# Two low-rank inputs transposed later in the projection phase, and modulation weights fetched one chunk earlier

## The chip, the core and the metric

The kernel runs on one core of one Trainium2 chip. The metric is device microseconds from start to end of one execution. The core has five instruction queues that run side by side, each strictly in its own order: PE (TensorE, matrix products and transposes), DVE (VectorE), ACT (ScalarE), POOL (GpSimd) and SP (SyncE, which here only issues transfers). They wait for one another through semaphores.

## What is computed

Two layers of a transformer over 512 latent tokens and 256 context tokens (768 rows, six tiles of 128) with 1024 features. The part that matters here is the input projection of a layer and what is made of its columns:

```
h  = modulate(rms_norm(x, g_norm_attn[l]), sh1, sc1)
lat = prep_stream(h @ w_in[l], rope_mla, rope_hd, *group_params)
# in prep_stream:
q_lat, kv_lat, k_pe, sq, sk, sv, dq, dk, dv, ga, gb, gc = split_columns(proj)
mq = (rms_norm(q_lat, g_q_lora) @ w_uq)
kv = (rms_norm(kv_lat, g_kv_lora) @ w_ukv)
sq = rms_norm(sq, g_swa_q); sk = rms_norm(sk, g_swa_k)      # then rope
dq = rms_norm(dq, g_diff_q); dk = rms_norm(dk, g_diff_k)    # then rope
```

After it come attention in three branches, a gated merge and an MLP. In the second (last) layer only the 512 latent rows are queries, so four tiles, not six, are made of each query group. The modulation vectors are `silu(c) @ w_mod + b_mod`.

## The kernel before

All products are kept at float32 accuracy by splitting each factor in a high and a low part and adding three products, so each (tile, 128-row slice of the weights) costs three matrix instructions. `piece` fetches weights into a staging tile `wr` (two buffers, on SP), ACT writes the high part `wh` (L197) and POOL the low part `wl` (L201). `bproj` (L473) runs the three products (L483, L484, L485) into an accumulator `pb`; ACT copies each finished tile out.

Each layer's phase 1 first computes the narrow columns, among them `rkv` (kv_lat) and `rq` (q_lat). Then `lora(rkv)` and `lora(rq)` are written in the code, ahead of all further chunks: ACT squares the rows (L464), DVE sums them (L465), forms the inverse root in some ten small dependent instructions (L445 to L456), scales the rows (L470); PE transposes the tiles into `pt` (L612; six to each 128 columns in the first layer for `rkv`, twelve for `rq`; six and eight in the second layer); ACT and DVE split the result into `lh` and `ll` (L615, L616). `kvT` and `qT`, these results, are what the low-rank products of `ukv` and `uq` read.

After that a string (L762) gives the order of the chunks, one letter each:

- a, c, g, i, m, n are `qk_chunk`: 256 columns of the big projection, 24 matrix instructions to a tile (144 for six tiles, 96 for four), then on DVE a sum of squares, the rotation with POOL's help (L505 to L512), the inverse root and the scaling, then a store to memory.
- e, k are `dvc`, the same size with no work after it. b, h, f, l are `ukv`: 3 instructions to a tile, 18 in all, reading `kvT`. d, j are `uq`: 6 instructions of 384 columns to a tile, reading `qT`.
- P starts the next phase (attention), whose first transposes `tp` read tiles `ld` that were stored and fetched back (`km`, `qm`).

In the first layer `mod_units(2)` runs after every letter: it fetches two weight tiles `wm` (SP, L308) and at once multiplies them (`pm`, L268) into a shared accumulator; every second call ends a group, which ACT copies (`me`), PE transposes (L276) and DVE adds up (L316).

The order on each engine is not the order of the code. A scheduler sets it ahead of time, from priorities that follow the order of the code and from tile dependencies; the code's order decides which instruction comes first where several are ready in its model, and in which order accumulator buffers are handed out. Accumulators `pb` alternate between two tags of two buffers each; `pt` and `pm` share a tag of two buffers. On the chip each engine then follows its fixed order: a waiting instruction holds up all behind it.

Of the kernel before, what the change touches and what calls it, by code (L numbers as in the profile page):

```python
# [14 lines left out]
F32 = mybir.dt.float32  # L15
# [30 lines left out]
P_GA, P_GM, P_BM, P_GQ, P_GKV, P_GS = 0, 8, 16, 64, 66, 67  # L46
# [90 lines left out]
class Build:  # L137
# [161 lines left out]
    def mod_units(self, n):  # L299

        nc = self.nc
        for _ in range(n):
            if self.mu == 24:
                return
            u, i = self.mu // 4, self.mu % 4
            self.mu += 1
            w = self.ph.tile([128, 1024], F32, tag="wm", bufs=self.NM, name=self.nm("wm"))
            nc.sync.dma_start(w, self.ins["wm1"][u, i])  # L308
            if i == 0:
                self.mps = self.psS("pm")  # L310
            self.mod_pe(w, (2 * i, 2 * i + 1), self.mps)
            if i == 3:
                v = self.mod_out(self.mps, self.mps[:, 512:640])
                o = (2, 4, 3)[u // 2] * 8 + u % 2 * 4
                for s in range(2):
                    nc.vector.scalar_tensor_tensor(out=self.mod[0][s][:, o:o + 4], in0=v[:, :, s], scalar=0.5,  # L316
                                                   in1=self.vp[0][:, P_BM + o:P_BM + o + 4], op0=ALU.mult, op1=ALU.add)
# [197 lines left out]
    def phase1(self, l, h, nq, pre):  # L515
# [102 lines left out]
                res.append((hi, lo))  # L618
            return res

        kvT = lora(rkv, 1, 6, P_GKV)

        ss = self.sumsq(rsk, 12, 64)
        self.rope_pairs(rsk, 1, 6, tabs["sk"], gains["sk"])
# [42 lines left out]
                nc.sync.dma_start(d, raw[:, a * nt * 128:(a + 1) * nt * 128])  # L667
                sc.setdefault(key, []).append(d)

        qT = lora(rq, 2, nq, P_GQ)  # L670

        kw = []

# [85 lines left out]
                 h=lambda: ukv(1), i=lambda: qk_chunk(2, qt, "sq", "qs"), j=lambda: uq(1), k=lambda: dvc(8),  # L759
                 l=lambda: ukv(3), m=lambda: qk_chunk(3, qt, "dq", "qd"), n=lambda: qk_chunk(4, qt, "dq", "qd"))  # L760

        for f in ("mcafldebghijnPk", "abcdjehmflgnikP")[l]:  # L762
            if f == "P":
                self.early = True
                for _ in job[0]():
                    pass
                self.early = False
                continue
            F[f]()
            if l == 0:  # L770
                self.mod_units(2)
# [591 lines left out]
    def build(self):  # L1363
        tc, nc, ins = self.tc, self.nc, self.ins
        import contextlib
        with contextlib.ExitStack() as es:
            self.kp = es.enter_context(tc.tile_pool(name="kp", bufs=1))
            self.sp = es.enter_context(tc.tile_pool(name="sp", bufs=1))
            self.pp = es.enter_context(tc.tile_pool(name="pp", bufs=1, space=bass.MemoryType.PSUM))
            self.dr = es.enter_context(tc.tile_pool(name="dr", bufs=1, space=bass.MemoryType.DRAM))  # L1370
            self.NS, self.WR, self.WH = 25, 2, 4
            kp = self.kp
            self.kc = kp.tile([128, NK], F32, name="kc")
            self.ident = self.kc[:, K_ID:K_ID + 128]
            self.vp, self.vb, self.mod, self.modr, self.lam, self.gsub, self.sink = [], [], [], [], [], [], []
            for l in range(DEPTH):
                self.vp.append(kp.tile([128, NP_], F32, name=f"vp{l}"))
                self.mod.append([kp.tile([128, 48], F32, name=f"mod{l}{s}") for s in range(2)])
                self.modr.append([kp.tile([128, 48], F32, name=f"modr{l}{s}") for s in range(2)])

            nc.scalar.preload_act_table_set("exp_and_others")

            cp, ct = self.tiny("cp", 64)[:, 0:16], self.tiny("cq", 64)[:, 0:16]
            nc.sync.dma_start(cp, ins["cp"])
            nc.scalar.activation(out=ct, in_=cp, func=AF.Tanh, scale=0.5)
            sl = self.sl = kp.tile([128, KT, 32], F32, name="sl")
            nc.vector.memset(sl, 0.0)
            nc.vector.scalar_tensor_tensor(out=sl[:, :, 0:2], in0=ct.rearrange("p (k s) -> p k s", s=2), scalar=1.0,
                                           in1=cp.rearrange("p (k s) -> p k s", s=2), op0=ALU.add, op1=ALU.mult)
            nc.sync.dma_start(self.kc[:, 0:K_COS], ins["kc"][:, 0:K_COS])  # L1390
            self.identr = kp.tile([128, 128], F32R, name="identr")
            nc.scalar.activation(out=self.identr, in_=self.ident, func=AF.Copy)
            nc.sync.dma_start(self.vp[0], ins["vp"][0])
            x = []
            for k in range(KT):
                t = self.S("x")
                nc.sync.dma_start(t, ins["xT"][k])
                x.append(t)
            xd = [ins["xT"][k] for k in range(KT)]
            with self.phase("p0", NPB=3):  # L1400
                h = self.norm_tiles()
                qps = self.first_norm(x, h)
            nc.sync.dma_start(self.kc[:, K_COS:NK], ins["kc"][:, K_COS:NK])
            nc.sync.dma_start(self.vp[1], ins["vp"][1])
            for l in range(DEPTH):
                nq = 6 if l < DEPTH - 1 else 4
                n = nq * 128
                with self.phase("p1", ND=5, NPB=3, NM=2):
                    self.layer_consts(l)
                    if l == 0:  # L1410
                        self.mu = 0
                    sc, job, st = self.phase1(l, h, nq, qps if l == 0 else pre)
                m = [None] * 8
                with self.phase("p2", ND=4, NPB=4, NL=3, NR=6, NG=3):
                    ys, gates = self.phase2(l, h, sc, nq, job, st)
                    yh = self.y_split(ys, 0, n)
                    yh = self.merge(l, 0, ys, yh, gates, m, nq, self.psd)
                with self.phase("p3", NR=16, NPB=2, NL=2, NG=4, NM=1):
                    yh = self.merge(l, 1, ys, yh, gates, m, nq, self.psx)
                    mh = self.merge(l, 2, ys, yh, gates, m, nq, self.psx)  # L1420
                    if l == 0:
                        self.silu = []
                        for s in range(2):
                            cb, t = (self.tiny(q, 64)[:, 0:8] for q in ("cb", "ct"))
                            nc.sync.dma_start(cb, ins["cc"][s].rearrange("(p q) -> p q", q=8))
                            nc.scalar.activation(out=t, in_=cb, func=AF.Tanh, scale=0.5)
                            nc.vector.scalar_tensor_tensor(out=t, in0=t, scalar=1.0, in1=cb, op0=ALU.add, op1=ALU.mult)
                            d = self.dr.tile([1024], F32, name=f"silu{s}")
                            nc.sync.dma_start(d.rearrange("(p q) -> p q", q=8), t)
                            self.silu.append(d)  # L1430
                    x = []
                    for k in range(KT):
                        t = self.S("x")
                        nc.sync.dma_start(t[:, :n], xd[k][:, :n])
                        x.append(t)
                    h2 = self.norm_tiles()
                    pre = self.out_proj(l, mh, x, nq, lambda acc, c: self.norm(l, 1, x, acc, h2, c, l == 0 and c.start >= LAT))
                with self.phase("p4", NR=16, NPB=3, NM=2):
                    if l == 0:
                        self.mod_start([(0, 5, (0, 1)), (1, 1, (0, 1)), (1, 0, (0, 1))]  # L1440
                                       + [(1, kd, (0,)) for kd in (2, 4, 3, 5)])
                        acc = self.S("acc1")
                        hn = self.norm_tiles()
                        xd = [self.dr.tile([128, 512], F32, name=self.nm("xd")) for _ in range(KT)]

                        def fin(j, c):
                            sq = self.ph.tile([128, 1024], F32, tag="wm", bufs=self.NM, name=self.nm("sq"))
                            self.add_square(acc, x[j], j, c, sq, nc.vector if j > 5 else nc.gpsimd)
                            if c.stop == LAT:
                                nc.sync.dma_start(xd[j], x[j][:, 0:LAT])  # L1450

                        def done(c):
                            self.norm(1, 0, x, acc, hn, c)
                    else:
                        def fin(j, c):
                            nc.sync.dma_start(self.out[j][:, c], x[j][:, c])

                        def done(c):
                            pass
                    pre = self.mlp(l, h2, x, nq, pre, fin, done)  # L1460
                    if l == 0:
                        h = hn
# [69 lines left out]
```

## Time and profile before

| | |
|---|---|
| median of three runs | 2515.46 us (2514.19 to 2516.1) |
| profiled execution | 2519.05 us, span of its instructions 2517.3 us |
| PE busy | 2425.4 us, 96% of the span |
| DVE, ACT, POOL busy | 60%, 43%, 44% |
| mean granted TensorE clock | 0.992 |
| phase 1, first layer | about 60 to 300 us |
| phase 1, second layer | about 1497 to 1700 us |

Times in the trace are counted from the span's first instruction. "Idle before" in brackets is how long the engine had stood still when that instruction began, and after the arrow what it waited for. Windows give each engine's busy time in a stretch and the granted clock as a share of full speed (1.00 is 2.4 GHz).

### The profile page before, as it was taken

The page shows a single profiled execution, that of the slowest core. Times are in us where ns is not written, and L with a number is a line of the kernel's source. Part 1 is how long each engine was busy: PE and PEld are TensorE (multiplying, and loading weights), DVE is VectorE, ACT ScalarE, POOL GpSimd, SP SyncE. Part 2 cuts the span into 40 slices and gives each one's busy share as a digit, 9 for nine tenths or more (in the row PEclk, how much of TensorE's full clock was granted, in tenths as well). Part 3 has the DMA queues.
Part 4 walks back from the last instruction along what each step waited for, and adds up shares of the span by engine and source line. Part 5 has one row for each costly group of instructions (what it writes and reads, how often), then busy time and mean ns, then how long its engine had stood idle before and what let it go on. Part 6 is the DMA issues. An engine that isn't in the chain of part 4 may idle for free. (4 is left out here: it accounts for less than half of the span.)

```text
span 2517.3 us, 40953 instructions
## 1 busy us (share of the span) xinstructions
PE 2425.4 (96%) x15466; PEld 2132.4 (85%) x15466; DVE 1498.0 (60%) x3081; ACT 1078.8 (43%) x2105; POOL 1102.9 (44%) x1423
## 2 busy tenths in 40 slices
PE   7999999999999999899999989999999999999999
PEld 6899888888888888788888889988888778888888
DVE  5547677778883468872222266777788874522222
ACT  4344466667662233222222234446677643422221
POOL 3534321221116438664444464562222247556654
PEclk9999999999999999999999999999999999999999
DMA  7265422222336315671111122542323354222222
GB/s 277 97 209 209 140 96 92 82 79 96 103 131 213 126 66 176 212 250 68 59 68 61 66 84 90 193 145 90 115 79 111 118 170 161 84 100 93 93 100 84
DMA packets 133190, 307.45 MB, mean 122 GB/s; under 512 B 43264, under 2 KB 49536, under 8 KB 132608
## 3 DMA queue, kind: packets, MB, share of 16 engines
q1 hardware_dynamic: 122624, 281.23, 32.9%
q10 hardware_dynamic: 10368, 23.60, 2.4%
q8 instruction: 122, 2.00, 0.3%
q14 instruction: 76, 0.62, 0.1%
HBM read 252.08 MB, written 52.70 MB: 121 GB/s over the span
## 5 line engine op out<-in xcount | busy, mean ns | idle before, releaser
L201 POOL TENSOR_TENSOR wl<-wr,wh 128x256 fp32r<-128x256 f32 x1060 | 847.2, 828 | 1014.5 <-ACT wh L197 959.4
L197 ACT ACTIVATE wh<-wr 128x1024 fp32r<-128x1024 f32 (+2 forms) x266 | 279.9, 1052 | 629.6 <-PE mo L221 310.0
L220 PE MATMUL mo<-uh,wh 128*128 128x512 f32 (+1 forms) x832 | 285.7, 343 | 15.6 <-DVE x L1263 12.6
L221 PE MATMUL mi<-hl,wh 128*128 128x512 f32 (+1 forms) x832 | 284.8, 343 | 0.9 <-DVE hl L436 0.9
L220 PE MATMUL mi<-hh,wh 128*128 128x512 f32 (+1 forms) x832 | 284.5, 343 | 0.9 <-ACT hh L435 0.4
L222 PE MATMUL mi<-hh,wl 128*128 128x512 f32 (+1 forms) x832 | 284.7, 343 | 0.0
L221 PE MATMUL mo<-ul,wh 128*128 128x512 f32 (+1 forms) x832 | 283.1, 340 | 0.0
L222 PE MATMUL mo<-uh,wl 128*128 128x512 f32 (+1 forms) x832 | 282.4, 340 | 0.0
L1309 DVE TENSOR_TENSOR ul<-u,uh 128x512 fp32r<-128x512 f32 (+1 forms) x104 | 96.1, 926 | 296.4 <-POOL u L1308 291.4
L1263 DVE SCALAR_TENSOR_TENSOR x<-mo,mod,x 128x512 f32<-128x512 f32 (+1 forms) x208 | 127.8, 624 | 203.2 <-PE mo L222 203.2
L484 PE MATMUL pb<-wl,hh 128*128 128x256 f32 (+1 forms) x832 | 243.5, 293 | 2.0 <-POOL wl L201 1.8
L483 PE MATMUL pb<-wh,hh 128*128 128x256 f32 (+1 forms) x832 | 243.9, 293 | 1.6 <-ACT rq L575 1.4
L485 PE MATMUL pb<-wh,hl 128*128 128x256 f32 (+1 forms) x832 | 243.5, 293 | 0.0
L220 PE MATMUL g<-hh,wh 128*128 128x512 f32 (+1 forms) x576 | 212.6, 369 | 0.0
L222 PE MATMUL g<-hh,wl 128*128 128x512 f32 (+1 forms) x576 | 212.4, 369 | 0.0
L221 PE MATMUL g<-hl,wh 128*128 128x512 f32 (+1 forms) x576 | 212.1, 368 | 0.0
L870 ACT ACTIVATE pth<-pT 128x512 fp32r<-128x512 f32 (+3 forms) x344 | 154.2, 462 | 91.1 <-PE pT L867 80.1
L220 PEld LDWEIGHTS mo<-uh,wh 128*128 128x128 f32 x832 | 156.7, 188 | 36.1 <-DVE x L1263 14.0
L871 DVE TENSOR_TENSOR ptl<-pT,pth 128x512 fp32r<-128x512 f32 (+3 forms) x344 | 171.7, 516 | 25.8 <-ACT pth L870 23.8
L220 PEld LDWEIGHTS mi<-hh,wh 128*128 128x128 f32 x832 | 156.3, 188 | 21.4 <-ACT hh L435 0.9
L221 PEld LDWEIGHTS mi<-hl,wh 128*128 128x128 f32 x832 | 156.6, 188 | 21.0 <-DVE hl L436 1.1
L222 PEld LDWEIGHTS mi<-hh,wl 128*128 128x128 f32 x832 | 156.6, 188 | 19.8
(243 smaller groups left out, 5859.0 us busy)
## 6 DMA issues: line engine op xcount, KB each, us to landing
wr<-in_wmi SPq DMA_DIRECT2D x64, 512.0 KB, 3.5
wr<-in_wmo SPq DMA_DIRECT2D x64, 512.0 KB, 3.5
wm<-in_wmod SPq DMA_DIRECT2D x56, 512.0 KB, 3.7
wr<-in_wg SPq DMA_DIRECT2D x48, 512.0 KB, 3.5
wr<-in_wb SPq DMA_DIRECT2D x36, 512.0 KB, 3.6
wm<-in_wm SPq DMA_DIRECT2D x28, 512.0 KB, 4.6
wr<-in_wup SPq DMA_DIRECT2D x24, 512.0 KB, 3.5
gd<-gt ACTq DMA_DIRECT2D x24, 384.0 KB, 2.4
```

Source lines behind the costliest of these rows:

```text
L197: nc.scalar.activation(out=hi[:, :n], in_=raw[:, :n], func=AF.Copy)
L201: nc.gpsimd.tensor_tensor(out=lo[:, c], in0=raw[:, c], in1=hi[:, c].bitcast(F32), op=ALU.subtract)
L220: mm(ps, lhsT=wh, rhs=xh[:, c], start=i == 0, stop=False)
L221: mm(ps, lhsT=wh, rhs=xl[:, c], start=False, stop=False)
L222: mm(ps, lhsT=wl, rhs=xh[:, c], start=False, stop=i == n - 1)
L483: mm(ps[:, :n], lhsT=ah[:, cs], rhs=wh, start=k == 0, stop=False)
L484: mm(ps[:, :n], lhsT=ah[:, cs], rhs=wl, start=False, stop=False)
L485: mm(ps[:, :n], lhsT=al[:, cs], rhs=wh, start=False, stop=k == nk - 1)
L870: nc.scalar.activation(out=hv[:, k0:k0 + n, qs], in_=pv, func=AF.Copy)
L871: nc.vector.tensor_tensor(out=lv[:, k0:k0 + n, qs], in0=pv, in1=hv[:, k0:k0 + n, qs].bitcast(F32), op=ALU.subtract)
L1263: self.nc.vector.scalar_tensor_tensor(out=x[j][:, c], in0=ps, scalar=g, in1=x[j][:, c], op0=ALU.mult, op1=ALU.add)
L1309: nc.vector.tensor_tensor(out=b[:, c], in0=u, in1=a[:, c].bitcast(F32), op=ALU.subtract)
```

## The change

`kvT` and `qT` are now made inside the chunk loop: two new letters K and Q call `lora` at their place in the string. In the first layer K follows chunk m and Q follows c; in the second K follows a, and Q follows c, which now stands ahead of b. `mod_units` fetches the pair of weight tiles for the next call and multiplies the pair fetched by the call before; the ring of `wm` grows from two tiles to four.

```
     def mod_units(self, n):
         nc = self.nc
-        for _ in range(n):
-            if self.mu == 24:
-                return
+        now, self.mw = self.mw, []
+        for k in range(n):
+            if self.mu + len(now) + k < 24:
+                w = self.ph.tile([128, 1024], F32, tag="wm", bufs=self.NM, name=self.nm("wm"))
+                nc.sync.dma_start(w, self.ins["wm1"][(self.mu + len(now) + k) // 4, (self.mu + len(now) + k) % 4])
+                self.mw.append(w)
+        for w in now:
             u, i = self.mu // 4, self.mu % 4
             self.mu += 1
-            w = self.ph.tile([128, 1024], F32, tag="wm", bufs=self.NM, name=self.nm("wm"))
-            nc.sync.dma_start(w, self.ins["wm1"][u, i])
...
-        kvT = lora(rkv, 1, 6, P_GKV)
+        kvT, qT = [], []
...
-        qT = lora(rq, 2, nq, P_GQ)
...
-        for f in ("mcafldebghijnPk", "abcdjehmflgnikP")[l]:
+        for f in ("mKcQafldebghijnPk", "aKcQbdjehmflgnikP")[l]:
+            if f == "K":
+                kvT += lora(rkv, 1, 6, P_GKV)
+                continue
+            if f == "Q":
+                qT += lora(rq, 2, nq, P_GQ)
+                continue
...
-                with self.phase("p1", ND=5, NPB=3, NM=2):
+                with self.phase("p1", ND=5, NPB=3, NM=4):
...
-                        self.mu = 0
+                        self.mu, self.mw = 0, []
```

Where the scheduler puts the moved steps shows in the order of the engines. First layer, PE, before: the transposes of `rkv` stand inside chunk m (`pb_1088` is its fourth tile), and those of `rq` further on in the same chunk.

```order
L484 MATMUL pb_1088<-wl_995,hh_110 128x256
L485 MATMUL pb_1088<-wh_993,hl_111 128x256
L612 MATMUL pt_890<-kc,rkv_652 128x128 x4
L612 MATMUL pt_897<-kc,rkv_652 128x128 x2
L483 MATMUL pb_1088<-wh_993,hh_112 128x256
```

The same engine after: the transposes of `rkv` stand in chunk c (`pb_1281` is its fifth tile), with 116 products of c ahead of them. Those of `rq` stand in chunk a.

```order
L487 MATMUL pb_1281<-wh_1169,hl_119 128x256
L485 MATMUL pb_1281<-wh_1169,hh_120 128x256
L486 MATMUL pb_1281<-wl_1171,hh_120 128x256
L614 MATMUL pt_1146<-kc,rkv_652 128x128 x4
L614 MATMUL pt_1153<-kc,rkv_652 128x128 x2
L487 MATMUL pb_1281<-wh_1169,hl_121 128x256
```

Chunk m thus runs without a transpose in it. Second layer, PE, before: the eight transposes of `rq` stand inside b (`pb_17137` and `pb_17142` are two of its six tiles, reading `lh_16862`, the split `kvT`), and chunk c (`pb_17211`) follows.

```order
L485 MATMUL pb_17137<-wh_17114,ll_16863 128x256
L612 MATMUL pt_16939<-kc,rq_16446 128x128 x4
L612 MATMUL pt_16948<-kc,rq_16446 128x128 x4
L483 MATMUL pb_17142<-wh_17114,lh_16862 128x256
L484 MATMUL pb_17142<-wl_17116,lh_16862 128x256
L485 MATMUL pb_17142<-wh_17114,ll_16863 128x256
L483 MATMUL pb_17147<-wh_17114,lh_16862 128x256
L484 MATMUL pb_17147<-wl_17116,lh_16862 128x256
L485 MATMUL pb_17147<-wh_17114,ll_16863 128x256
L483 MATMUL pb_17211<-wh_17194,hh_11188 128x256
```

The same engine after: c is done by then, b's last tile (`pb_17358`) ends, the transposes of `rq` follow, and behind them come at once the first products of d (`pb_17412` and on), which read the result of the transposes, `lh_17305`.

```order
L487 MATMUL pb_17353<-wh_17325,ll_17061 128x256
L485 MATMUL pb_17358<-wh_17325,lh_17060 128x256
L486 MATMUL pb_17358<-wl_17327,lh_17060 128x256
L487 MATMUL pb_17358<-wh_17325,ll_17061 128x256
L614 MATMUL pt_17307<-kc,rq_16446 128x128 x4
L614 MATMUL pt_17316<-kc,rq_16446 128x128 x4
L485 MATMUL pb_17412<-wh_17405,lh_17305 128x384
L486 MATMUL pb_17412<-wl_17407,lh_17305 128x384
```

Chunk c, 144 products, has moved from behind the transposes of `rq` to ahead of them. On DVE in the second layer, before, the scaling of `rq` stands ahead of chunk a's own chain (`ss_17079` is a's first step, and chunk c comes after a).

```order
L456 SCALAR_TENSOR_TENSOR y_16922<-a_16923,y_16922 128x4
L470 TENSOR_TENSOR rq_16446<-rq_16446,y_16922 128x1024
L465 TENSOR_REDUCE ss_17079<-sqs_17078 128x16
L616 SCALAR_TENSOR_TENSOR ll_16938<-pt_16939,vp_72,lh_16937 128x512
L507 TENSOR_TENSOR raw_16973<-raw_16973,tab_16410 128x512
```

After, it stands behind the scaling of chunk c (`raw_17092`), and also behind b's first sum (`v_17369` is formed from it).

```order
L447 TENSOR_SCALAR v_17369<-ss_17364 128x24
L472 TENSOR_TENSOR raw_17092<-raw_17092,y_17266 128x1536
L458 SCALAR_TENSOR_TENSOR y_17290<-a_17291,y_17290 128x4
L451 TENSOR_SCALAR y_17370<-v_17369 128x24
L456 TENSOR_TENSOR a_17291<-y_17290 128x4
L453 TENSOR_SCALAR y_17370<-y_17370 128x24
L457 SCALAR_TENSOR_TENSOR a_17291<-a_17291,v_17289 128x4
L456 TENSOR_TENSOR a_17371<-y_17370 128x24
L458 SCALAR_TENSOR_TENSOR y_17290<-a_17291,y_17290 128x4
L457 SCALAR_TENSOR_TENSOR a_17371<-a_17371,v_17369 128x24
L472 TENSOR_TENSOR rq_16446<-rq_16446,y_17290 128x1024
```

So the whole work on chunk c now stands between c's products and the scaling of `rq`. On SP in the first layer, before, the first two `wm` tiles are fetched ahead of chunk c's weights and the next two behind them:

```order
L308 DMA wm_1202<-in_wm 128x1024
L308 DMA wm_1213<-in_wm 128x1024
L1425 DMA cb_10400<-in_cc 128x8
L1429 DMA silu_10405<-ct_10401 128x8
L1425 DMA cb_10407<-in_cc 128x8
L1429 DMA silu_10412<-ct_10408 128x8
L194 DMA wr_1223<-in_wb 128x1024
```

After, four stand there:

```order
L306 DMA wm_1120<-in_wm 128x1024
L306 DMA wm_1122<-in_wm 128x1024
L306 DMA wm_1369<-in_wm 128x1024
L306 DMA wm_1371<-in_wm 128x1024
L1433 DMA cb_10400<-in_cc 128x8
L1437 DMA silu_10405<-ct_10401 128x8
```

Later pairs stand one chunk earlier in SP's queue than before. The order of POOL is the same in both, and outside phase 1 of each layer (and the first steps of the first layer's phase 2) so is that of every engine.

## Rows read from the trace of the kernel before

**Rows 1.** The page: busy time of each engine.
```profile
PE 2425.4 (96%) x15466; PEld 2132.4 (85%) x15466; DVE 1498.0 (60%) x3081; ACT 1078.8 (43%) x2105; POOL 1102.9 (44%) x1423
```

**Rows 2.** Windows: stretch, length; busy PE, PEld, DVE, ACT, POOL; clock; DMA share, GB/s.
```profile
60.00:300.00 240.00, 226.72 (x1948) 214.61 (x1947) 146.30 (x343) 92.80 (x190) 107.39 (x153) 0.98 0.49 171
300.00:500.00 200.00, 199.19 (x1354) 173.80 (x1353) 152.76 (x357) 133.56 (x310) 38.48 (x58) 1.00 0.26 89
```

**Rows 3.** Timeline of PE, first layer: start, length, instruction, [idle before <- waited for].
```profile
95.49 0.88 PE L612 MATMUL pt<-kc,rkv 128*128 128x128 f32 x6 [2.54 <-DVE rkv L470]
...
103.95 1.32 PE L612 MATMUL pt<-kc,rq 128*128 128x128 f32 x6 [2.72 <-DVE rq L470]
...
109.90 1.08 PE L268 MATMUL pm<-wm,sl 128*32 128x128 f32 x32
...
129.20 0.38 PE L483 MATMUL pb<-wh,hh 128*128 128x256 f32 x1
...
154.98 0.76 PE L268 MATMUL pm<-wm,sl 128*32 128x128 f32 x16 [2.10 <-DMA wm<-in_wm]
...
192.73 0.64 PE L268 MATMUL pm<-wm,sl 128*32 128x128 f32 x16 [1.43 <-DMA wm<-in_wm]
```

**Rows 4.** Windows of five us, columns as in rows 2.
```profile
105.00:110.00 5.00, 5.00 (x37) 4.86 (x39) 2.17 (x4) 2.95 (x6) 0.00 (x0) 0.74 0.02 3
...
155.00:160.00 5.00, 5.00 (x35) 4.69 (x36) 2.63 (x16) 1.92 (x5) 0.00 (x0) 0.66 0.40 158
...
1505.00:1510.00 5.00, 4.00 (x10) 3.18 (x10) 1.67 (x4) 0.00 (x0) 5.00 (x16) 0.50 0.00 0
...
1550.00:1555.00 5.00, 2.43 (x19) 2.02 (x19) 4.59 (x6) 2.94 (x7) 5.00 (x7) 1.00 0.27 79
```

**Rows 5.** Timeline of DVE, first layer: chunks m and c, first sum and scaling.
```profile
112.87 1.75 DVE L465 TENSOR_REDUCE ss<-sqs 128x24 f32<-128x1536 f32 x1 [2.76 <-ACT sqs L464]
...
121.30 1.76 DVE L470 TENSOR_TENSOR raw<-raw,y 128x1536 f32<-128x1536 f32 x1
...
130.82 1.75 DVE L465 TENSOR_REDUCE ss<-sqs 128x24 f32<-128x1536 f32 x1 [7.76 <-ACT sqs L464]
...
138.48 1.76 DVE L470 TENSOR_TENSOR raw<-raw,y 128x1536 f32<-128x1536 f32 x1
```

**Rows 6.** Timeline of PE, second layer.
```profile
1535.38 0.28 PE L483 MATMUL pb<-wh,hh 128*128 128x256 f32 x1
...
1545.43 0.87 PE L612 MATMUL pt<-kc,rkv 128*128 128x128 f32 x6 [1.11 <-DVE rkv L470]
...
1552.64 1.09 PE L612 MATMUL pt<-kc,rq 128*128 128x128 f32 x8 [2.31 <-DVE rq L470]
...
1571.90 0.34 PE L483 MATMUL pb<-wh,lh 128*128 128x384 f32 x1
...
1580.75 0.39 PE L483 MATMUL pb<-wh,hh 128*128 128x256 f32 x1 [0.24 <-ACT rl L724]
...
1614.96 0.39 PE L483 MATMUL pb<-wh,lh 128*128 128x256 f32 x1 [1.21 <-ACT rawkv L681]
...
1686.46 0.84 PE L782 MATMUL tp<-identr,ld 128*96 128x128 f32 x6 [5.75 <-DMA ld<-km]
```

**Rows 7.** Timeline of ACT, second layer, behind the last tile of chunk c.
```profile
1572.38 1.05 ACT L197 ACTIVATE wh<-wr 128x1024 fp32r<-128x1024 f32 x1
1573.33 1.48 ACT L464 ACTIVATE sqs<-raw 128x1536 f32<-128x1536 f32 x1
```

**Rows 8.** Timeline of DVE, second layer: the chain of `rq`, and chunk c's.
```profile
1543.06 1.22 DVE L465 TENSOR_REDUCE ss<-sqs 128x4 f32<-128x1024 f32 x1
...
1550.88 1.71 DVE L470 TENSOR_TENSOR rq<-rq,y 128x1024 f32<-128x1024 f32 x1
...
1574.84 1.75 DVE L465 TENSOR_REDUCE ss<-sqs 128x24 f32<-128x1536 f32 x1 [1.83 <-ACT sqs L464]
...
1593.14 1.75 DVE L470 TENSOR_TENSOR raw<-raw,y 128x1536 f32<-128x1536 f32 x1
```

## The prediction

> **What bounds the kernel now.** Read the busy times first [rows 1]: PE is busy 2425.4 of 2517.3 us, so PE's own order sets the end and only its idle 92 us, or time at a low clock, can be won. Windows then tell where the idle time lies [rows 2]: from 300 to 500 us PE is idle for 0.8 us of 200, from 60 to 300 us (phase 1 of the first layer) for 13.3 us of 240. A microsecond won or lost on PE in phase 1 therefore reaches the end whole, unless a later wait takes it up. The timeline of PE names the waits that the change touches: 2.54 and 2.72 us ahead of the transposes of `rkv` and `rq`, 2.10 and 1.43 us ahead of modulation products whose weights had not landed [rows 3]; in the second layer 1.11 and 2.31 us ahead of the same transposes [rows 6]. The clock: of 105 to 110 us at 0.74 and 155 to 160 us at 0.66 [rows 4], with the two levels 1.0 and 0.5, 2.6 and 3.4 us ran at half speed, a loss of half of that, 1.3 and 1.7 us.
>
> **Sum, first layer.** The most there is to win is 2.54 + 2.72 + 2.10 + 1.43 + 1.3 + 1.7 = 11.8 us. Against that stand the waits that appear in the new places.
>
> Chunk m then has no transposes in it and ends some 9.2 us earlier than its 109.90 [rows 3], near 100.6: the two waits and the clock (6.6 us) are gone, and its 18 transposes (0.88 us for six at full clock, so some 2.6) come later, a shift and no gain. On DVE the chain of m, from first sum to the end of the scaling, is 121.30 + 1.76 - 112.87 = 10.2 us and starts 3.0 us after m's last product [rows 3, 5]. It will run from 103.6 to 113.8, and the rest of the `rkv` chain, a sum and a scaling of some 0.95 us each, of which the sum can lie inside it, ends near 115.7. PE comes to the transposes after 116 products of c. A product takes 0.12 us: from 109.90 to 129.20 lie the 144 of c and two batches of `pm` at some 1.0 us [rows 3]. That is 100.6 + 13.8 = 114.4, so a new wait of 1.3 us; c ends at 119.8 and a starts at 120.8 in place of 129.20. For `rq`: c's DVE chain is 138.48 + 1.76 - 130.82 = 9.4 us [rows 5], from 122.4 to 131.8; a sum and a scaling of 1.76 each and small steps take it to 135.9, and PE is there at 134.7: a wait of 1.2 us. The `rq` transposes now share two accumulators with a `pm` group that holds one, so 0.5 to 1 us of small waits. The weights are asked for one chunk, some 20 us, ahead, but where a chunk is short (f, d) the request sits on SP behind stores that wait for DVE: I leave 0 to 1.5 us of the 3.53 us standing. Sum: 11.8 - 1.3 - 1.2 - 0.8 = 8.5 with nothing left of the `wm` waits; I take **-8.5 us**, with a range of -5 (waits that stay, or a new half-clock stretch) to -11 (no new wait for the transposes).
>
> **Sum, second layer.** Here the string moves c ahead of b, and Q behind c. Chunk a starts at 1535.38 [rows 6] and, 96 products later, ends at 1546.9; c takes 144 x 0.12 = 17.1 us. The transposes of `rkv` stand 95 products into c, near 1558.2, and wait for a's DVE chain and `rkv`'s, until about 1561: a wait of 0 to 3 us, 2.9 taken. c ends near 1567.7. Behind it b has only 18 products, 2.2 us; ACT does a weight part and the square of c first (1.05 and 1.48 us, [rows 7]), and the square of `rq`, before it empties b's accumulators, so b stalls for 2.6 us and ends near 1572.5. (Its like today is the 1.21 us at 1614.96 [rows 6].) Next on PE are the transposes of `rq`, and everything behind them reads their result. DVE's order has the scaling of `rq` behind all of c's chain. That chain starts after c's last copy, weight part and square, near 1570.4. Its length has two bounds. From below it is the 9.4 us of the first layer [rows 5]; with the sum of `rq` (1.22 us, [rows 8]), the first sum of b (1.75, as c's), the scaling of `rq` (1.2) and 0.9 of small steps that makes 14.5. From above it is the same chunk in the second layer, 1593.14 + 1.75 - 1574.84 = 20.1 us [rows 8], of which some 7.2 is work for d and j that lies between (two sums of 1.75, four rotation steps of 0.7, small steps), so 12.9; with the scaling of `rq` at 1.71 [rows 8] and the rest as before, 18.5. I take 16, nearer the lower end, since POOL, which slows DVE's steps there, has less to do once PE stands still. The scaling ends near 1586.4 where PE arrived at 1572.5: **a wait of about 14 us**, where today's is 2.31. The transposes take 1.1 us, ACT's part 0.7; seven products of d can go ahead of DVE's part `ll`, which stands behind the scaling of b (1.75) and seven small steps and comes at about 1590.4. The other 41 of the 48 products of d and j need 41 x 0.18 = 7.4 us, from 8.85 us for all [rows 6], so e starts near 1597.8 in place of 1580.75: **+17 us**, and the two waits of today are in it already. Range +13 (lower chain, no wait for `rkv`) to +21.
>
> The clock after that wait: today 4.16 us of idling before 1505.46 went with a clock of 0.50 for the five us that follow, and a wait of 2.31 us with none lost [rows 4, 6]. So some us of d at half clock are likely, and 1 us is in the upper end, none in the 17, because in the first of them `ll` is the later.
>
> The Trainium skill has a page, TensorE: Matmul & The Clock Gate (section HAM oscillation — how this bites in real kernels), which says that every stretch of waiting that lets the clock drop is paid for again afterwards by products at half speed. The trace agrees at 155 to 160 us (0.66). By it the sum would be some 1 to 2 us higher than mine; this speaks against the new long wait, and nothing above rests on it.
>
> **The total.** -8.5 + 17 = +8.5. The profiled execution took 2519.05 us, 3.6 us more than the median of 2515.46; the difference is carried over to the median: 2515.5 + 8.5 = **2524 us**, 0.34% slower. About 0.2%, 5 us, is what a measurement of this kernel can tell from no change.
>
> **Rivals.** First, *the second layer's loss is given back later*, which ends faster. While PE stands still, DVE, ACT and SP catch up, so waits behind e may shrink: the 1.21 us at 1614.96, and above all the 5.75 us at 1686.46, where attention waits for a `km` tile fetched back [rows 6]. All of that, with some 2 us of clock, is 9 us. With the best of the first layer (-11) and the least of the second (+13) it gives -7, 2508.5 us. For it: DVE starts e with c's chain done, which it had not. Against it: that fetch stands on SP behind stores and weight loads that follow PE's own chunks, so it moves along with PE. It decides only if more than 7 of the 9 us go. Chance 0.10.
>
> Second, *the wait is near its lower bound*: DVE runs c's chain as fast as in the first layer, and the first layer gives its most. Then -9.5 + 13 = +3.5, 2519 us, not to be told from no change. Chance 0.22, with the partly given-back cases.
>
> Third, *the loads don't arrive in time, and DVE is slowed by POOL throughout*: first layer -5, second +20, so +15, 2530.5 us. For it: the 12.9 us of c's chain with POOL at work. Chance 0.18.
>
> That the change does not do what it says in the second layer (c's work not ahead of `rq`'s) is ruled out by the fixed order of DVE.
>
> **How the numbers follow.** Forecast case, 2521 to 2528 us: 0.50. With the third, and a bit of the second's upper half, slower by over 0.2% has 0.68; within 0.2% 0.21; faster 0.11. For 8 in 10 the range leaves out 0.1 on either side: from 2512 to 2531.
>
> **What would show it.** In the profile after: PE with no wait for `rkv` or `rq` before 105 us; waits of 1 to 1.5 us for both between 113 and 137 us; no or short waits for `wm`; a's first product near 120.8. In the second layer: a wait of 12 to 16 us ahead of `pt<-rq`, put down to DVE's scaling of `rq`, and the first product of e some 15 to 19 us later than before, less the first layer's gain. I am wrong if that wait is under 8 us, if the scaling of `rq` runs before c's chain, or if the 5.75 us wait at the end of the phase is gone.

## The result

The changed kernel takes 2536.26 us (median of 4 runs, 2534.77 to 2538.06) where the kernel before took 2514.82 on the same chip: 21.4 us more, a ratio of 1.008 with a 95% interval of 1.0067 to 1.0093. The sign was right, the size was not: 8.5 us were forecast, and the range ended at 2531.

The profiled execution has a span of 2534.8 us, 17.5 more than before. (The rest of the 21.4 is that the profiled execution of before lay 4 us over its median.) Three places on PE's timeline divide these 17.5 us. First, PE's last wait ahead of the second layer, the same instruction in both kernels, before and after:

```profile
1485.98 0.39 PE L220 MATMUL mo<-uh,wh 128*128 128x256 f32 x1 [0.34 <-DVE nt L433]
```
```profile
1485.24 0.39 PE L220 MATMUL mo<-uh,wh 128*128 128x256 f32 x1 [0.34 <-DVE nt L435]
```

In these two executions the whole first layer has given 0.74 us, where 8.5 were forecast. The second place is attention's first transpose in the second layer, at 1702.68 for 1686.46 [rows 6]: +16.2, so the second layer's phase 1 has cost 17.0 us, as forecast. From there to the end another 1.3 are lost, with PE in the same order in both.

**First layer.** PE's timeline after (start, length, instruction, idle before and what it waited for), to be read against [rows 3]:

```profile
117.41 0.87 PE L614 MATMUL pt<-kc,rkv 128*128 128x128 f32 x6 [3.22 <-DVE rkv L472]
...
140.73 0.66 PE L614 MATMUL pt<-kc,rq 128*128 128x128 f32 x4 [2.41 <-DVE rq L472]
...
162.42 0.65 PE L268 MATMUL pm<-wm,sl 128*32 128x128 f32 x16 [0.88 <-DMA wm<-in_wm]
...
267.36 0.84 PE L790 MATMUL tp<-identr,ld 128*96 128x128 f32 x6 [4.95 <-DMA ld<-km]
```

The waits for weights have shrunk from 3.53 to 0.88 us. But the waits ahead of the transposes are there again in the new places, 3.22 and 2.41 us for 2.54 and 2.72, and the wait of attention for a fetched `km` tile at the end of the phase has grown to 4.95 us. Before it was:

```profile
270.71 0.59 PE L782 MATMUL tp<-identr,ld 128*96 128x128 f32 x6 [2.25 <-DMA ld<-km]
```

How far the changed kernel is ahead can be read by pairing the instructions of PE that have the same place in both orders: 5.1 us where the kernel before stands at 260 us, and 0.95 us where it stands at 330 us. So there was a gain until attention's first fetched tiles, and 4.2 us of it went there.

**Second layer**, against [rows 6]:

```profile
1560.24 1.54 PE L614 MATMUL pt<-kc,rkv 128*128 128x128 f32 x6 [4.21 <-DVE rkv L472]
...
1573.53 0.38 PE L485 MATMUL pb<-wh,lh 128*128 128x256 f32 x1 [2.59 <-ACT rawkv L682]
...
1586.09 1.97 PE L614 MATMUL pt<-kc,rq 128*128 128x128 f32 x8 [11.59 <-DVE rq L472]
...
1597.36 0.28 PE L485 MATMUL pb<-wh,hh 128*128 128x256 f32 x1
...
1702.68 0.85 PE L790 MATMUL tp<-identr,ld 128*96 128x128 f32 x6 [5.61 <-DMA ld<-km]
```

The three waits of the forecast are there, 4.21 (2.9 forecast), 2.59 (2.6) and 11.59 (14), and e's first product is at 1597.36 (1597.8 forecast). What stands ahead of the transposes of `rq` shows on DVE: c's first sum, c's scaling, then that of `rq`.

```profile
1572.29 1.75 DVE L467 TENSOR_REDUCE ss<-sqs 128x24 f32<-128x1536 f32 x1 [9.04 <-ACT sqs L466]
...
1582.33 1.75 DVE L472 TENSOR_TENSOR raw<-raw,y 128x1536 f32<-128x1536 f32 x1
...
1584.81 1.22 DVE L472 TENSOR_TENSOR rq<-rq,y 128x1024 f32<-128x1024 f32 x1
```

Windows of five us (columns as in rows 2) show PE standing, and its clock during the waits and behind them:

```profile
1560.00:1565.00 5.00, 4.76 (x23) 4.76 (x24) 1.33 (x3) 1.32 (x3) 2.15 (x4) 0.50 0.15 57
...
1575.00:1580.00 5.00, 0.00 (x0) 0.00 (x0) 4.90 (x18) 1.44 (x1) 0.00 (x0) 0.62 0.29 102
1580.00:1585.00 5.00, 0.00 (x0) 0.00 (x0) 5.00 (x22) 0.00 (x0) 0.00 (x0) 0.50 0.01 6
1585.00:1590.00 5.00, 3.91 (x15) 3.59 (x16) 4.76 (x11) 1.37 (x2) 0.00 (x0) 0.51 0.39 152
```

From 1575 to 1590 us DVE is busy nearly throughout, POOL not at all.

### The profile page after: what moved, and what is told of

It is laid out like the page before. It is cut to its first block, busy times and chain, and to the rows that moved or that the text cites. A ratio compares the mean times of both kernels' runs of the same rounds, so it can differ in the third digit from the quotient of the medians.

```text
span 2534.8 us, 40948 instructions
## 1 busy us (share of the span) xinstructions
PE 2426.7 (96%) x15466; PEld 2135.0 (84%) x15466; DVE 1488.0 (59%) x3081; ACT 1079.3 (43%) x2105; POOL 1089.6 (43%) x1423
## 5 line engine op out<-in xcount | busy, mean ns | idle before, releaser
L201 POOL TENSOR_TENSOR wl<-wr,wh 128x256 fp32r<-128x256 f32 x1060 | 833.2, 815 | 1027.7 <-ACT wh L197 962.0
L220 PE MATMUL mo<-uh,wh 128*128 128x512 f32 (+1 forms) x832 | 285.9, 344 | 16.2 <-DVE x L1271 12.9
```

The source lines that it names most:

```text
L201: nc.gpsimd.tensor_tensor(out=lo[:, c], in0=raw[:, c], in1=hi[:, c].bitcast(F32), op=ALU.subtract)
L220: mm(ps, lhsT=wh, rhs=xh[:, c], start=i == 0, stop=False)
```

## The experiments

Each time is given against runs of the kernel before on the same chip, whose medians lay between 2517.8 and 2518.5 us. The expectations call the experiments by short names; each is given here.

**One part at a time.** The change with the second layer put back (e1):

```
-        for f in ("mKcQafldebghijnPk", "aKcQbdjehmflgnikP")[l]:
+        for f in ("mKcQafldebghijnPk", "abcdjehmflgnikP")[l]:
...
+        if l == 1:
+            kvT += lora(rkv, 1, 6, P_GKV)
```

(`qT` likewise, both at their old places.)

> The change with only the second layer put back: its lora calls at their old place and its old order of chunks; the first layer and the earlier weight fetch as changed. Theory (the second layer's order of chunks costs some 16 us, because the scaling of rq stands behind chunk c's work on DVE; the first layer's gain is mostly taken back at its end): no wait over 3 us ahead of the second layer's transposes, and a time 0 to 3 us under the kernel before. Rival (the loss comes from the first layer or the weight fetch, through SP or the clock): 10 us or more above the kernel before.

Measured: 2522.84 us, ratio 1.0017 (1.0006 to 1.0028), so 4 to 5 us over the kernel before. Neither theory nor rival: far under the rival's 10, but not the small gain either. PE's waits in the first layer (line waited for: sum, times, longest):

```profile
PE tp L794 <- DMA ld<-km: 5.5, 1, 5.5
PE pt L614 <- DVE rkv L472: 3.1, 1, 3.1
PE pt L614 <- DVE rq L472: 2.9, 1, 2.9
```

The first layer's part of the change is a small loss, not a gain of 8.5. That is the step that failed. Paired as above, this run was 2.3 us ahead at 260 us, 2.4 behind at 330 and 3.3 behind at 1485, where the profiled execution of the change, with the same first layer, was 0.74 ahead: single executions of one order differ by some 4 us here.

The kernel before with only the second layer changed (e2), `("mcafldebghijnPk", "aKcQbdjehmflgnikP")`, with both calls of `lora` in the loop for that layer:

> The kernel before with only the second layer's order of chunks and lora calls as changed. Theory: waits of about 4 us (rkv) and 11 to 12 us (rq) ahead of the second layer's transposes, and 16 to 20 us above the kernel before. Rival: under 8 us above it.

Measured: 2537.66 us, ratio 1.0078 (1.0052 to 1.0104), 19.6 us over. Its waits are the changed kernel's:

```profile
PE pt L612 <- DVE rq L470: 10.9, 1, 10.9
...
PE pt L612 <- DVE rkv L470: 4.2, 1, 4.2
```

The second layer's order is nearly all of the loss. 4.5 and 19.6 us together are 24, near the 21.4 of both.

The kernel before with only the new `mod_units` and the ring of four (e3), the strings and `lora` calls as before:

> The kernel before with only the earlier weight fetch and the ring of four. The two waits for weights (2.10 and 1.43 us) and a stretch at half clock (1.7 us) should go. Theory (a gain in the first layer's projection phase is mostly taken back where attention waits for a fetched tile at 270 us): 0 to 2.5 us under the kernel before, the wait there longer than 2.25 us. Rival (it carries to the end): 4.5 to 6 us under.

Measured: 2521.61 us, ratio 1.0011 (0.9998 to 1.0024): not to be told from no change, and on the side of a loss. The waits for weights are gone. At the same instruction of PE's order the run was 3.4 us ahead of the kernel before at 160 us, 4.8 at 260 and 0.3 at 330: between the last two stands

```profile
PE tp L794 <- DMA ld<-km: 6.0, 1, 6.0
```

where the kernel before waits 2.25 us. So in the trace the gain of this part is taken back as the theory had it; the time measured is a little worse than expected.

The kernel before with only the first layer's K and Q moved (e4), `("mKcQafldebghijnPk", "abcdjehmflgnikP")`, the fetch as before:

> The kernel before with only the first layer's lora calls moved, as in the change; the weight fetch and the second layer as before. Theory (issued late, the sums and the scaling of rkv and rq stand behind chunk work on DVE, and the waits only move): waits of 2 to 3.5 us ahead of both groups of transposes, the waits for weights still there, and 0 to 6 us above the kernel before. Rival (the moved transposes gain, and the fetch takes it back): 3 us or more under the kernel before.

Measured: 2521.46 us, ratio 1.0015 (1.0003 to 1.0027), 3.7 us over. The waits moved and did not shrink, and those for weights stayed:

```profile
PE pm L268 <- DMA wm<-in_wm: 4.0, 4, 1.4
PE pt L612 <- DVE rkv L470: 3.2, 1, 3.2
PE pt L612 <- DVE rq L470: 2.8, 1, 2.8
PE tp L792 <- DMA ld<-km: 2.1, 1, 2.1
```

**The place of the scaling.** `lora` is cut in two. The sums and the scaling stay where they were in the code, ahead of all chunks; only the transposes and what follows go to K and Q:

```
         def lora(raw, kts, nt, gcol):
-            ss = self.sumsq(raw[:, :nt * w], nt, w)
-            r = self.rsq_small(ss, nt, w)
-            self.scale_rows(raw[:, :nt * w], r, nt, w)
...
         kvT, qT = [], []
+        lnorm(rkv, 1, 6)
...
+        lnorm(rq, 2, nq)
```

(`lnorm` holds the three lines taken out above.)

In both layers, all else as in the change (e5):

> The change with lora cut in two: the sums and the scaling of rkv and rq are issued at their old place in the code, ahead of all chunks, and only the transposes with what follows at K and Q. Theory (the waits come from DVE's order, not from the place of the transposes): no wait over 0.5 us ahead of any of these transposes, 20 to 30 us under the change, 3 to 10 us under the kernel before. Rival (c ahead of b and the place of Q cost by themselves, in buffers or ACT): above the kernel before.

Measured: 2524.42 us, ratio 1.0023 (1.0012 to 1.0033): 6 us over the kernel before, where the change is 21 over, so some 15 us better than the change. The theory was right on the waits and wrong on the time. All waits ahead of these transposes are 0.4 us or less, and the run is 11.7 us ahead of the kernel before at 260 us, 8.2 at 330 and 7.4 at 1475: the first layer's gain is there, and most of it carries that far. But in the second layer PE now waits at e (timeline of PE, then of ACT):

```profile
1582.69 0.58 PE L485 MATMUL pb<-wh,hh 128*128 128x256 f32 x1 [7.70 <-ACT rl L730]
```
```profile
1580.78 1.48 ACT L466 ACTIVATE sqs<-rl 128x1536 f32<-128x1536 f32 x1 [9.19 <-DVE ko L712]
```

PE needs j's accumulators emptied. On ACT j's copies (`rl`, L730) stand behind the square of d's result, and that square waits for DVE to end its work on b, which stands behind c's. Behind the late scaling there was a second cause of nearly the same size.

**The order of the chunks alone.** The kernel before with `"acbdjehmflgnikP"` in the second layer (f4), c ahead of b and both `lora` calls at their old place:

> The kernel before with only c ahead of b in the second layer, both lora calls at their old place. Theory (the order of the chunks is the cause by itself): idle time of PE of 7 to 11 us between the end of c and e's first product, and 8 to 13 us above the kernel before. Rival (the late scaling of rq is the cause): within 3 us of the kernel before.

Measured: 2529.66 us, ratio 1.0048 (1.0033 to 1.0063), 11 us over, as the theory had it:

```profile
1577.56 0.44 PE L483 MATMUL pb<-wh,lh 128*128 128x384 f32 x1 [2.31 <-ACT rl L727]
...
1589.24 0.58 PE L483 MATMUL pb<-wh,hh 128*128 128x256 f32 x1 [7.19 <-ACT rl L727]
```

So c ahead of b costs 11 to 12 us by itself, and the late scaling with its transposes behind a and c adds some 8 to make 19.6. The two are not a sum of two waits: in the changed kernel the wait for `rq` gives DVE the time that it needs for b, so the wait at e does not appear.

Six instead of five of the shared wide buffers, on top of that (h1, `ND=5` to `ND=5 if l == 0 else 6`):

> As f4 (only c ahead of b in the second layer), with six buffers instead of five in that layer for the wide tiles that raw, rawkv, rl, ko and the squares share. In f4 ACT stood for 8.0 us ahead of the square of d's result until DVE's last step on b freed such a buffer, and PE's wait of 7.2 us hung on that. Theory (the chunks' order makes DVE late, and the shared buffers pass that on to PE): the 7.2 us wait falls under 4 us, and 3 to 8 us under f4 (2529.7 us, or 11 us over the kernel before on its chip). Rival (PE waits for DVE's results whatever buffers there are): within 2 us of f4, the wait over 6 us.

Measured: 2527.72 us, ratio 1.0035 (1.0022 to 1.0047). The wait at e went from 7.19 to 5.93 us, and ACT no longer stands at d's square, but a step on, at the copies of j's tiles, for the same step of DVE:

```profile
1588.52 1.64 ACT L727 ACTIVATE rl<-pb 128x384 f32<-128x384 f32 x4 [7.28 <-DVE ko L707]
```

Neither expectation was met in full: one more buffer takes 1.3 us off the wait, since the next user of a buffer waits for the same work, and the intervals of the two times overlap. What is late is DVE. Whether still more buffers would hide it was not tried and stays open.

K behind a and Q behind b, with b left ahead of c, `"aKbQcdjehmflgnikP"` on the kernel before (f3). The expectation says Q behind c; in the string it stands ahead of it:

> The kernel before with only the second layer's K behind a and Q behind c, but b still ahead of c, as it was. Theory (it is c ahead of b that makes the long waits, since b, d and j alone can't cover DVE's work on c): a wait under 4 us ahead of the transposes of rq, and 0 to 5 us above the kernel before. Rival (the scaling of rq behind other work on DVE is the cost, wherever b stands): 10 us or more above it.

Measured: 2534.88 us, ratio 1.0071 (1.0056 to 1.0086), 16 us over. The theory failed on the time, and the timeline says how:

```profile
1561.77 0.48 PE L612 MATMUL pt<-kc,rkv 128*128 128x128 f32 x1 [15.34 <-DVE rkv L470]
...
1585.96 0.48 PE L612 MATMUL pt<-kc,rq 128*128 128x128 f32 x1 [2.52 <-DVE rq L470]
```

The wait for `rq` is 2.5 us, as expected under 4: its scaling has only b's work ahead of it on DVE, not c's, and 127 products of c stand ahead of its transposes on PE. But b, which reads `kvT`, now follows a at once, and the scaling of `rkv` stands behind a's whole chain on DVE: the same wait at the other letter. In both kernels a scaling issued behind a chunk waits for that chunk's work on DVE, and shows as a wait of PE unless enough other products stand ahead of its reader. Since nothing was issued behind c here, the theory itself, that b ahead of c would keep the wait behind c short, stays untested.

**The first layer mended.** Second layer as in the kernel before; in the first, `lora` cut in two as above, with the transposes at K and Q, and the new fetch (f1):

> The second layer as in the kernel before; in the first layer the sums and the scaling of rkv and rq are issued ahead of all chunks, and only the transposes with what follows stand at K and Q; the earlier weight fetch is in. Theory (the first layer loses its gain to waits for DVE that follow from issuing the scaling late; without them it carries to the end): no wait over 0.5 us ahead of the first layer's transposes, and 4 to 8 us under the kernel before. Rival (the first layer's gain is taken back by attention's wait for a fetched tile, whatever is done earlier): within 2 us of the kernel before.

Measured: 2514.78 us, ratio 0.9987 (0.9975 to 0.9999): 3.7 us by the medians, 3.3 by the ratio, under the expected 4 to 8. Against e1, which differs in the first layer by the place of the sums and the scaling alone and was 4 to 5 us over, that place is worth some 8 us. The profiled execution, 4 us under the median, has the transposes' waits gone and is 11.7 us ahead at 260 us and 7.8 at 330, but this wait is still there:

```profile
PE tp L799 <- DMA ld<-km: 4.5, 1, 4.5
```

The same with the old fetch, `mod_units` and `NM=2` as before (f2):

> As f1, with the weight fetch as in the kernel before. Theory (waits for weights of 2.10 and 1.43 us come back): 2 to 5 us over f1, 1 to 5 us under the kernel before. Rival (the fetch is worth nothing, as in the run with the fetch alone): within 1 us of f1.

Measured: 2517.07 us, ratio 0.9996 (0.9985 to 1.0007). The fetch is worth 2.3 us here, at the lower end of the expected; the two intervals overlap. Against e4, again with the place of the sums and the scaling as the only difference, it is some 5 us better, with intervals that just overlap.

In the changed kernel, SP's timeline ahead of that wait reads

```profile
259.15 1.77 SPq L747 DMA_DIRECT2D qm<-rc  x4
261.06 0.85 SPq L194 DMA_DIRECT2D wr<-in_wg  x2
262.32 0.33 SPq L800 DMA_DIRECT2D ld<-km  x1
```

The last store of these tiles (`km`) had gone out by 226 us; the fetch stands behind the stores of j (`qm`), whose last ones wait 3.7 us for DVE, and behind two fetches of weights. So j is moved right behind d, `("mKcQafldjebghinPk", "abcdjehmflgnikP")`, on top of f1 (g1):

> As f1 (only the transposes moved in the first layer, fetch earlier, second layer as before), and in the first layer j stands right behind d, so that its eight stores no longer stand on SP between i's stores and the fetch of the tile that attention waits for at 260 us. Theory (that wait of 4.5 us is SP's queue held up by stores of work that DVE has not done yet): the wait under 1.5 us, and 3 to 6 us under f1, so 7 to 11 us under the kernel before. Rival (the wait is for i's chain on DVE itself or for loads): 3 us or more of it stay.

Measured: 2511.59 us, ratio 0.9978 (0.9968 to 0.9988), 6 us under the kernel before and the lowest time of all versions. No wait for `km` is left. But the fetch did not go out earlier than in f1. In f1, on SP and then on PE:

```profile
254.92 0.33 SPq L809 DMA_DIRECT2D ld<-km  x1
```
```profile
260.33 0.85 PE L799 MATMUL tp<-identr,ld 128*96 128x128 f32 x6 [4.52 <-DMA ld<-km]
```

In g1:

```profile
252.43 3.56 SPq L194 DMA_DIRECT2D wr<-in_wg  x2
256.33 0.33 SPq L809 DMA_DIRECT2D ld<-km  x1
```
```profile
260.59 0.55 PE L799 MATMUL tp<-identr,ld 128*96 128x128 f32 x6
```

With j's stores out of the way, the fetch stands behind two fetches of weights, of which the second waits 2.9 us for POOL to have used its buffer, and goes out 1.4 us later than in f1. The transposes start at the same time. The wait is gone because PE comes to them later: it is 7.2 us ahead of the kernel before at 260 us, where f1 is 11.7, having lost 2.95 us at 188 us to a new wait for ACT's copy of a finished tile `rawkv`, with the clock at 0.80 and 0.86 in the ten us from 185 us on. So the wait is under 1.5 us as the theory had it, but its reason, j's stores as what holds the fetch up, is not shown. Without the standstill the clock stays at 1.00 from 260 to 270 us, where it was 0.50 and 0.95 in f1, and at 330 us g1 is 8.4 us ahead for f1's 7.8. In time g1 is 2 to 3 us under f1, a little less than expected, and the two intervals overlap.

With P ahead of k in the second layer too (g3), `"abcdjehmflgniPk"`:

> As g1, and in the second layer attention's first steps (P) stand ahead of the last chunk k, as they do in the first layer. Theory (the wait of 5.75 us there is the fetch's place behind k's stores): that wait under 3 us, and 3 to 7 us under g1. Rival (it waits for i's chain on DVE): within 1.5 us of g1.

Measured: 2525.29 us, ratio 1.0034 (1.0022 to 1.0046), 14 us worse than g1. Theory and rival both fail:

```profile
1658.39 0.58 PE L485 MATMUL pb<-wh,hh 128*128 128x256 f32 x1 [4.16 <-ACT raw L660]
1672.86 0.88 PE L799 MATMUL tp<-identr,ld 128*96 128x128 f32 x6 [6.10 <-DMA ld<-km]
```

The wait for `km` stays, and comes earlier, with less of k's work behind it done. On SP that fetch, at 1668.70 us, stands right behind two fetches of weights that take from 1660.98 to 1668.61; that these are what makes it late was not tested.

## Why the prediction was right and wrong

**What bounds the kernel**: right. PE's order sets the end, and what was lost in phase 1 of the second layer (17.0 us at 1702 us) reached the end whole. The first rival, that it is given back later, did not happen: the wait of 5.75 us stayed at 5.61.

**The second layer's term, +17**: right in its mechanism and size, by the trace (+17.0) and nearly so by the run of that part alone (19.6). Its parts erred against each other, so that the size fits so closely is in part luck: `rkv` 4.21 for 2.9, `rq` 11.59 for 14, and the clock, which was put at nothing, was 0.50 from 1560 to 1565 us, behind the wait for `rkv`, and 0.51 from 1585 to 1590, behind that for `rq`. Four of the first seven products of d took 0.52 us in place of 0.34 each, yet most of them ran while `ll` was still to come, as the sum had it. The chain on DVE took 13.7 us from c's first sum to the end of the scaling of `rq` (1572.29 to 1586.03), under the 14.5 of the lower bound: through the wait, with POOL idle from 1574 us on, its small steps took 0.15 to 0.18 us each, and the 16 was too long. The start was 2 us later than forecast, behind the longer wait for `rkv` and the half clock after it. What the sum did not see is that c ahead of b would have cost 11 us even without the late scaling.

**The first layer's term, -8.5**: this step failed. By that part alone (e1) it is +4 to +5 us, by the profiled execution -0.7. Of the 7.8 that the trace lacks, 3.4 were lost before 260 us and 4.2 between 260 and 330 us. Three pieces were mis-sized.

(1) The waits of 1.3 and 1.2 us for the transposes were 3.22 and 2.41. For `rkv`, PE came to the transposes at 114.2 us (114.4 forecast), and m's scaling ended at 113.7 (113.8 forecast). What stood behind that scaling on DVE was missed:

```profile
111.41 0.16 DVE L458 SCALAR_TENSOR_TENSOR y<-a,y 128x6 f32<-128x6 f32 x1
...
111.96 1.76 DVE L472 TENSOR_TENSOR raw<-raw,y 128x1536 f32<-128x1536 f32 x1
113.64 0.70 DVE L458 SCALAR_TENSOR_TENSOR y<-a,y 128x6 f32<-128x6 f32 x1
114.37 0.64 DVE L456 TENSOR_TENSOR a<-y 128x6 f32<-128x6 f32 x1
115.05 0.64 DVE L457 SCALAR_TENSOR_TENSOR a<-a,v 128x6 f32<-128x6 f32 x1
115.72 0.64 DVE L458 SCALAR_TENSOR_TENSOR y<-a,y 128x6 f32<-128x6 f32 x1
116.40 0.96 DVE L472 TENSOR_TENSOR rkv<-rkv,y 128x768 f32<-128x768 f32 x1
```

The sum let the scaling of `rkv` follow at once, with room for its sum of 0.95 us besides, and ended at 115.7. But four small steps of the inverse root, which it had not counted, were left, 2.8 us from the end of m's scaling to the start of that of `rkv`. The same steps had taken 0.16 us each just before. In between POOL had begun its part of chunk c's rotation, four instructions end to end, of which these are the first and the last:

```profile
112.32 1.99 POOL L507 TENSOR_TENSOR rt<-raw,tab 128x256 f32<-128x256 f32 x1 [6.03 <-ACT raw L654]
...
115.63 0.71 POOL L508 TENSOR_TENSOR rt<-raw,tab 128x256 f32<-128x256 f32 x1
```

At some 0.2 us for each step the wait would have been near 1.2 us, an estimate from these rows, close to the 1.3 of the forecast. The prediction had POOL slow DVE in the second layer, and left it out of the first. For `rq` it was the same: three steps of 0.59 to 0.66 us from 136.4 us on, while POOL worked, and a scaling of 2.24 us that began while it still did.

(2) Behind the wait the clock was down again, which the sum had taken as gone:

```profile
120.00:125.00 5.00, 5.00 (x58) 4.67 (x58) 0.00 (x0) 2.90 (x4) 2.55 (x4) 0.78 0.12 16
...
265.00:270.00 5.00, 2.64 (x11) 2.29 (x12) 4.45 (x13) 0.86 (x2) 0.00 (x0) 0.55 0.30 117
```

At 0.78 of five us, 2.2 ran at half speed, a loss of 1.1 in that window alone.

(3) The sentence that a microsecond won on PE in phase 1 reaches the end whole, unless a later wait takes it up, put the wait at the end of the phase at nothing. It went from 2.25 to 4.95 us, with the clock at 0.55 around its end. PE came to those transposes 6.0 us earlier than before (262.41 for 268.46: 5.1 that it was ahead, the rest because four products fewer stand ahead of them), and the fetch went out only 2.9 us earlier (262.32 for 265.20). DVE, for which the stores ahead of the fetch wait, was busy for 29.1 of the 30 us from 240 to 270 us (29.45 before). The next wait, for `qm`, was 1.49 us for 0.74 before. These make 3.5 of the 4.2 us lost there; the clock is some of the rest.

Of these three the runs show the first: the sums and the scaling issued early take the waits away, and the time falls by some 8 us (e1 and f1, whose intervals lie apart) or 5 (e4 and f2). At 260 us such a kernel is 11.7 us ahead, all of the 11.8 that the prediction named as the most there is to win. Yet only 3.3 to 3.7 us of that are left in the medians of f1, and 6 in g1. That the third takes the difference is read from traces; no run brought the fetch forward against PE's coming to it, and the cause stays open there.

**Rivals.** The third (first layer -5, second +20) was the nearest; the first layer's loss of all its gain lay outside it. The second took -9.5 for a first layer that gives its most, where the term's own bound is -11; nothing hangs on that. The range ended 5 us too low because its bounds for the first layer, -5 to -11, had no case in which that part turns to a loss.

The page TensorE: Matmul & The Clock Gate of the Trainium skill (section HAM oscillation — how this bites in real kernels) was weighed as some 1 to 2 us against the change. The trace agrees in kind, with windows at 0.50, 0.51 and 0.55 at the ends of the new waits and behind them; the profiled executions don't separate its price from the waits themselves.

## What to carry to other kernels

When a step is moved to a later place in the code, look at which of its instructions have to move. Here only the transposes were to come later; the sums and the scaling went with them, behind a chunk's whole work on DVE, and turned a wait of 2.3 us into one of 11.6. And before a gain on the bounding engine is carried to the end, find the next wait behind it that another engine's backlog or a queue's order sets, and ask whether that moves too.

## What was not expected of the hardware

Small dependent steps on DVE (128 x 4 to 128 x 24 elements) took 0.15 to 0.18 us each where POOL was idle, and 0.6 to 0.7 us in stretches where POOL ran. In the first layer of the changed kernel the change falls together with POOL's start at 112.32 us. In f3 it shows on both sides: POOL works from 1580.40 to 1583.24 us, four steps of 128 x 4 from 1580.60 to 1583.27 took 0.59 to 0.67 us each, and the steps right behind them 0.16. The link is read from such stretches and was not tested by itself.

Stretches between 330 and 1485 us and behind 1750 us, where PE's order is the same, differed between some of the profiled executions by 2 to 4 us, some of it in stretches at half clock that one had and another had not; medians of the kernel before lay between 2514.8 and 2518.5 us. Effects of 2 us in this kernel need more than a profile each.
